# Modulation products of the first layer in four (three) column groups of 32 instead of two

## The chip, the cores and the metric

The kernel runs on one core of one Trainium2 chip. The metric is the device time in microseconds (us) of that core for one whole execution; a smaller number is better. The engines are named as the profile names them: PE (TensorE's matmuls), PEld (its weight loads), DVE (VectorE), ACT (ScalarE), POOL (GpSimd) and SP, the engine on whose queue most transfers are issued, in the order in which they are written and each after the waits of its own. Numbers such as L72 are lines of the kernel before.

## The reference

Two trunk layers of a diffusion backbone run over 128 context tokens and 512 latent tokens, 1024 features each. What matters here is the first line of a layer: every layer makes from a condition vector of 1024 features (one for the context, one for the latents) six vectors of 1024 features that shift, scale and gate its activations. These are the modulation.

```
mod_ctx = silu(c_ctx) @ w_mod[l] + b_mod[l]
mod_lat = (silu(c) @ w_mod[l] + b_mod[l])[:, None, :]
...
shift1, scale1, gate1, shift2, scale2, gate2 = split(mod, 6)
h   = (x * (1 + scale1) + shift1) @ w_in
mix = [ RWKV-7 (4 heads) | neighbourhood attention (4 heads) | GQA (8 heads) ] @ w_out
x   = LN1(alpha * x + gate1 * mix)
x   = LN2(alpha * x + gate2 * ((silu(gate) * up) @ w_ffn_out))
```

`w_mod[l]` is a matrix of 1024 x 6144 in float32, so a modulation is a product of two rows with 48 blocks of 128 columns. The rest of a layer is a dense projection, three mixers (a chunked recurrent scan and two kinds of attention), an output projection and a gated feed-forward, all in float32 accuracy.

## The kernel before

Activations lie feature-major: 128 features on the partitions, the tokens in two chunks of 320 on the free axis. A dense product is made as three products of float32r parts (`mm3`: high x high, high x low, low x high). Weights come by SP's queue in blocks of 128 x 1024 floats (`weights`, L300; transfer L306), and ACT and DVE split them in two parts (`split`, L277 and L278). All of PE's products are recorded by one helper, `Tensor.matmul` (L72), transposes by L76.

The modulation of the first layer is made in three ways. The scale and the first two shift blocks, and what comes after block 40, are dot products on DVE (`mod_block`, L194). Blocks 2 to 7 and 16 to 39 are made by `mod` (L196), which this change is about. `mod(j0, n, ...)` makes n blocks. The stationary operand is `cst`, silu(c) with each of the two condition vectors repeated 16 times, so 128 features x 32 columns. The weights stream past it as the moving operand: for each of the eight slices k of 128 features a transfer of 128 x (128 n) floats (L203), and then two products, one for each half of the n blocks, that write to PSUM partitions 0 to 31 and 32 to 63 of one bank, `ps_pv`. After the eighth, ACT copies the bank to SBUF (L210), PE transposes it block by block (L76), and DVE adds the bias into `modT` (L217). One slice with its two products is called a step below.

`mod` is called with n = 6 in `first_input` (L352), where the input of the first layer is made feature tile by feature tile as its weights come in, and with n = 4 six times in `proj_all` (L435): twice beside the projection tiles of the scan's features, and four times beside those of queries, keys and values. So there are 8 steps of 2 x 384 columns and 48 steps of 2 x 256 columns, and nothing like them in the second layer. Each of PE's float32 products has two records in the profile, so a step has four.

The order of independent work is set as the program is written out. `Tensor.now` is a running estimate of PE's time, which each product raises by a formula of its size:

```
L68  if lhsT.dtype == F32R:
L69      self.now += n / 2400
L70  else:
L71      self.now += (max(n, 100) if out.shape[0] > CH else max(n, 80) * 0.55) / 600
```

Side work is written as generators (tasks), each of which yields the time from the end of its products to where it can go on. `tick` (L255) is called every few dense products, and emits one step of each task whose time has come by that estimate; `weave` (L267) emits the tasks by themselves, the one that is ready first going first. The steps of `mod`, the eight scan jobs of a layer (`rwkv_job`, L632, in two slots: elementwise features, products within chunks, the inverse of their 16 x 16 blocks, states) and the attention are such tasks. So when the estimate changes, the order of everything that is woven after it can change, up to the end of the layer's mixers. On top of that the framework fixes each engine's own instruction list, which the engine then runs in order.

The names that the prediction uses: `md` are the matrices of a scan job, written to DRAM by ACT's queue (`md<-X`) and read back by SP's queue as 16 x 16 blocks, `BT` (L723); DVE inverts these (L775 to L788), ACT writes the transposed result `td`, and SP's queue reads it as `T` (L797) and `X` (L799), each in two transfers, one for each of the job's two heads. PE then joins the blocks, first `A` x `T`. The digit behind BT, T or X is the slot. `bias` (L937), `vw` (L927), `ks` (L951) and `qs` (L944) are loads for the attention, into space that comes free when the last dense tile of the projection is done.

Of the kernel before, what the change touches and what calls it, by code (L numbers as in the profile page):

```python
# [60 lines left out]
class Tensor:  # L61
    """TensorE's products, with a running estimate of its time (us) that orders the emission of independent work"""
# [3 lines left out]
    def matmul(self, out, lhsT, rhs, **kw):  # L66
        n = math.prod(out.shape[1:])
        if lhsT.dtype == F32R:  # L68
            self.now += n / 2400  # L69
        else:  # L70
            self.now += (max(n, 100) if out.shape[0] > CH else max(n, 80) * 0.55) / 600  # L71
        self.eng.matmul(out, lhsT, rhs, **kw)  # L72
# [11 lines left out]
class Build:  # L84
# [3 lines left out]
    def t(self, shape, name, dt=F32):  # L88
        """short-lived tile of the present phase"""
        return self.tpool.tile(shape, dt, name=name, tag="t", bufs=self.tbufs)  # L90
# [4 lines left out]
    # ---------------------------------------------------------------- set-up  # L95
# [51 lines left out]
    def mat(self, t, h):  # L147
        """the 64 x 64 matrices of one head in DRAM scratch, row first"""
        return t[:, h, 0:CH * CH].rearrange("c (s t) -> s c t", t=CH)

    def blocks(self, t):
        """their diagonal 16 x 16 blocks, one to a partition: [(chunk, head, block), row, column]"""
        b = t[0, 0, 0:1]
        return bass.AP(tensor=b.tensor, offset=b.offset, ap=[[MP // 4, 4 * NC], [CH, 16], [1, 16]])

    # ------------------------------------------------------------ modulation
    def silu_c(self):
        """silu(c) with the features on the partitions, as the stationary operand of mod"""
# [8 lines left out]
    def silu_rows(self, pool, spread):  # L167
        """silu(c) on every partition, spread there by TensorE or by the load"""
# [20 lines left out]
    def mod_block(self, l, j, c, w):  # L189
        """128 columns of the modulation as dot products on VectorE"""  # L190
# [5 lines left out]
    def mod(self, j0, n, pool, bufs=2, width=4 * P):  # L196
        """n blocks of 128 columns of the modulation of the first layer as products with the weights streamed"""
        nc = self.nc
        ps = self.psum("pv")
        w0, nb = j0 * P, n // 2 * P  # L200
        for k in range(KT):
            w = pool.tile([P, width], F32, name="wmod", tag="wmod", bufs=bufs)
            nc.sync.dma_start(w[:, 0:2 * nb], self.I["w_mod"][k * P:(k + 1) * P, w0:w0 + 2 * nb])  # L203
            yield 1.5
            for j in range(2):
# [3 lines left out]
        sb = pool.tile([P, width], F32, name="wmod", tag="wmod", bufs=bufs)[0:CH, 0:nb]  # L209
        nc.scalar.copy(sb, ps[0:CH, 0:nb])  # L210
        yield 1.0
        pt = self.psum("pv")
        for b in range(n // 2):
            self.te.transpose(pt[:, b * CH:(b + 1) * CH], sb[:, b * P:(b + 1) * P], self.ident[0:CH, 0:CH])
        src = pt[:, 0:n // 2 * CH].rearrange("p (b j w r) -> p b j w r", j=2, w=2, r=16)
        for w in range(2):
            nc.vector.tensor_tensor(  # L217
                self.modT[0][:, j0:j0 + n, w].rearrange("p (j b) -> p b j", j=2),
                src[:, :, :, w, 0],
                self.par(0, "b_mod", j0, n).rearrange("p (j b) -> p b j", j=2), ALU.add)  # L220

    def coefs(self, l, which, ln):
        """scale/bias that turn the normalised (or, without ln, the plain) x into the modulated input"""
# [15 lines left out]
    # ------------------------------------------------------ tasks on the side  # L239
    # A task is a generator of emission steps; what it yields is the time (us) from the end of the step's products  # L240
    # to where its next step can start.
# [13 lines left out]
    def tick(self):  # L255
        """beside the dense products: one step of each task that is ready"""
# [4 lines left out]
    def drain(self, *tasks):  # L261
        """emit what is left of these tasks"""
# [4 lines left out]
    def weave(self, *tasks):  # L267
        """emit the tasks, the first to be ready first, until these (or all) are done"""
# [5 lines left out]
    def split(self, src, hi, lo, scale=1.0):  # L274
        """float32r parts of src, scaled by a power of two"""
# [7 lines left out]
    def psum(self, tag):  # L283
        """PSUM: s2 holds two banks; rw and pv one"""
# [3 lines left out]
    def head_sums(self, ps, col, x, ones, starts):  # L288
        """per token (on the partitions) and head: sums of x over the head's features, for 128 tokens from each start"""
# [3 lines left out]
    def head_spread(self, ps, v, blocks):  # L293
        """v of (token, head) to all features of the head; blocks: column of v, its first token, columns of ps"""
# [5 lines left out]
    def weights(self, dram, n=1024, tag="w", dst=None):  # L300
        """load a [128, n] block of weights and split it exactly in two float32r parts"""
# [15 lines left out]
    # -------------------------------------------------------------- main flow  # L317
# [34 lines left out]
    def first_input(self, pool):  # L352
        """modulated input of the first layer, a feature tile at a time, and its products in the first projection tiles"""
# [62 lines left out]
    # ---------------------------------------------------- projection + mixing  # L416
    def proj(self, l, mts):
        """feature-major projection tiles; yields the two PSUM parts of 320 tokens of each"""
# [52 lines left out]
    def mixed(self, l):  # L471
        """the mixers' outputs as the input of the output projection, whose first tiles run beside the last scans"""
# [16 lines left out]
    def rwkv_slot(self, l, slot, pool):  # L489
        """the jobs that one set of tiles carries; the next job's features are made while the states of the one  # L490
        before are scanned"""
# [18 lines left out]
    def conv(self, l, mts):  # L510
        """short convolution over the tokens of each group"""
# [21 lines left out]
    def sigmoid(self, dst, src, bias=0.0):  # L533
        """sigmoid as 0.5 tanh(x / 2) + 0.5 (same table set as exp); bias is already halved"""
        self.nc.scalar.activation(dst, src, AF.Tanh, bias=bias, scale=0.5)

    def rwkv_begin(self, l):
# [18 lines left out]
        # normalised removal keys  # L556
# [17 lines left out]
    def rwkv_pre(self, l, ft):  # L574
        """bonus into kds, gate into v"""
# [20 lines left out]
    def rwkv_end(self, l, ft, c):  # L596
        """group norm, bonus and gate of one half of the tokens"""
# [34 lines left out]
    def rwkv_job(self, l, ft, hb, d, slot, pool):  # L632
        """One scan of two heads over five chunks, in the scan's order (backward: time reversed). Four stages:
        element-wise features; within-chunk products; inverse of their blocks; states and outputs."""
# [12 lines left out]
        def features():  # L647
# [19 lines left out]
            # FT: rho, alpha, v, alpha ; BK: beta, kappa, beta  # L667
# [31 lines left out]
        def products():  # L699
            """[beta; kappa] x [rho | alpha] of each chunk (rows swapped for the odd head)"""  # L700
            FT_, BK, W = J.FT, J.BK, J.W
            # ST: the masked products with rho, and the decayed beta, kappa in time-major order
# [18 lines left out]
            # diagonal 16x16 blocks of M^T to one partition each  # L721
# [6 lines left out]
            # time-major alpha, V and the decayed beta, kappa  # L728
# [25 lines left out]
        def inverse():  # L754
            """inverse of the blocks: 8x8 row by row from the bottom, then two of them joined"""
# [7 lines left out]
            def q8(t, i, j0, j1):  # L763
                """row i, columns j0..j1 of both diagonal 8x8 blocks"""
# [3 lines left out]
            def q8m(t, i0, i1, j0, j1):  # L768
                """transposed view [q, j, i] of rows i0..i1, columns j0..j1 of both 8x8 blocks"""
# [32 lines left out]
        def bmm(lhs, rhs, N, evac, swap=False):  # L802
            """lhs^T rhs of both heads, chunk by chunk; swap: the operands lie on the other head's partitions"""
# [8 lines left out]
        def states():  # L812
# [4 lines left out]
            # R = N V, next to alpha  # L817
            bmm(N, lambda k, c, h: RV[k, c, h, :], CH, lambda ps, c: nc.scalar.copy(AL[:, c, CH:P], ps), True)
            yield 1.17
            # X = (I - M^T)^-1 by joining blocks 16 -> 32 -> 64; T = X^T  # L820
# [11 lines left out]
            # [A' | R'] = T [alpha | R]  # L832
# [8 lines left out]
            # rho' = rho + A'^T P^T ; G^T = A'^T beta^  # L841
# [6 lines left out]
            # states at the chunks' starts  # L848
# [49 lines left out]
    # ------------------------------------------------------------- attention  # L898
    # Scores are float32r products over the stacked parts: [qh; ql] x [kh; kh], then x [kl; kl].
    def bias_rows(self, l):  # L900
        """relative position bias: every row 16 times with pitch RP, read back with pitch RP - 1"""
# [18 lines left out]
    def na_values(self, l, ft):  # L920
        """values of the window of query block j, half of the rows each: partition = (row, column)"""
# [8 lines left out]
    def na_bias(self, l, hd):  # L930
        """bias of query (r, c) and window key (7 - r', c')"""
# [9 lines left out]
    def stacked(self, dram, h, name, n, bufs):  # L941
        """one head's parts on top of each other"""
# [4 lines left out]
    def doubled(self, dram, h):  # L947
        """one head's keys, each part on both halves of the partitions"""
# [16 lines left out]
    def na_qk(self, l):  # L965
# [5 lines left out]
        for ft in range(2):  # L971
            # latent queries in the order (column block, row, column)
# [10 lines left out]
        for ft in range(2):  # L983
            # latent keys, with the softmax's scale, from the last row of the grid to the first
# [13 lines left out]
    def rope(self, x, hi, dram):  # L998
        """x * cos + partner(x) * sin on [128, 512], its float32r parts into DRAM"""
# [10 lines left out]
    def gqa_qk(self, l):  # L1010
# [27 lines left out]
        # queries: weight and rotary here, 1/rms with the softmax's scale  # L1038
# [18 lines left out]
    def values(self, l):  # L1057
        """token-major values: na_v (4 heads) and gqa_v (2 heads)"""
# [52 lines left out]
    def softmax(self, ps, n, negmax, scale, sums=None):  # L1111
        """exp(scale * ps - max) on [128, n], over its sum unless that is asked for; returns the SBUF tile"""
# [12 lines left out]
    def normed(self, o, pv, sums, view):  # L1125
        """o = the outputs of four pairs of heads over the sums (query, block, head)"""
# [7 lines left out]
    def transposed(self, p, nb):  # L1134
        """nb blocks of 128 keys of the probabilities, keys on the partitions"""
# [47 lines left out]
    def na_pair(self, l, ft, j, qk, vw, st):  # L1183
# [33 lines left out]
        if j == 3:  # L1217
            o = self.out[2 + ft][0][:, NCTX:]
            yield 1.0
            # back to the order (row, column block, column)  # L1220
# [3 lines left out]
    def gqa_pair(self, l, kv, m, t, qs, ks, st):  # L1224
        """heads 4 kv + 2 m and the next one"""
# [32 lines left out]
    # ------------------------------------------- output projection, LN, FFN  # L1258
    def gated(self, l, which, mt, c, ps, xa, z):
        """z = gate * ps + xa on one chunk of 320 tokens"""  # L1260
# [8 lines left out]
    def sums(self, c, first, z):  # L1269
        """running sums over the features of z and z^2"""  # L1270
# [330 lines left out]
```

## Time and profile before

| what | us |
|---|---|
| median of three runs | 2216.33 |
| lowest and highest of them | 2186.16, 2217.32 |
| span of the profiled execution, first to last instruction | 2193.9 |
| PE busy in it | 2090.7 (95%) |
| DVE, ACT busy | 1286.8 (59%), 901.2 (41%) |

The profiled execution is one more execution of the same program; of it the profile gives the span, and no time for what lies around it. Stages by the span's clock: input of the first layer 0 to 65, projections with the modulation beside them 65 to about 293, the rest of the mixers to 587, output projection and feed-forward to about 1110, then the second layer. In the trace a wait is put beside the instruction that ended it, and the chain of waits follows the work that ended last back from the end.

### The profile page before, as it was taken

To read this page: it belongs to the slowest core of one execution; us is meant where nothing else is said; L and a number is where in the kernel's file an instruction comes from. 1 tells how busy PE (TensorE), PEld (TensorE's weight loads), DVE (VectorE), ACT (ScalarE), POOL (GpSimd) and SP (SyncE) were. 2 spreads that over 40 slices of the span, in tenths; PEclk is the share of its full clock that TensorE was granted. 3 is DMA by queue.
4 is the path that set the end of the run, shared out by engine and by line. 5 is a ranking of instruction groups with operands and counts; after the bars stand their busy time and mean duration, and the time that the engine had idled before them with its cause. 6 is when DMAs were issued, how large, how long until landed. Compare 5 with 4: busy or idle time off the path is not lost.

```text
span 2193.9 us, 41015 instructions
## 1 busy us (share of the span) xinstructions
PE 2090.7 (95%) x16705; PEld 1883.8 (86%) x16705; DVE 1286.8 (59%) x2786; ACT 901.2 (41%) x1807; POOL 188.3 (9%) x355
## 2 busy tenths in 40 slices
PE   6989998899999999999999999989999999999997
PEld 4867776678899999999988887667779999999997
DVE  6445667576676666666766567556667523333247
ACT  3534454554564212212465445445454521221234
POOL 0011131010100000000020223100101000000000
PEclk9999998899999999999999999789999999999998
DMA  8554354111323444444431425421013122122223
GB/s 293 149 164 152 108 106 82 47 31 31 138 75 133 147 154 150 148 140 147 141 130 68 133 72 103 86 60 27 22 54 130 58 73 82 68 72 82 71 86 113
DMA packets 186594, 226.43 MB, mean 103 GB/s; under 512 B 119061, under 2 KB 128917, under 8 KB 186277
## 3 DMA queue, kind: packets, MB, share of 16 engines
q1 hardware_dynamic: 150148, 206.72, 30.7%
q0 software_dynamic: 3984, 11.90, 1.7%
q10 hardware_dynamic: 32274, 5.20, 1.4%
q8 instruction: 131, 2.15, 0.4%
q14 instruction: 57, 0.47, 0.1%
HBM read 198.37 MB, written 25.40 MB: 102 GB/s over the span
## 4 chain that ended last, share of the span: by engine, by line
PE 79%; DMA 7%; DVE 5%; issue 4%; ACT 3%; SPq 1%; POOL 0%; ACTq 0%; POOLq 0%; DVEq 0%
PE ps_s L72 43%; PE ps_rw L72 28%; PE ps_pv L72 4%; PE ps_rw L76 4%; DMA wmod<-in_w_mod 2%; DMA td<-TB 2%; DMA qs<-nqd 1%; DMA BT<-md 1%; ACT whi L277 1%; DVE wlo L278 0%; DMA c_raw<-in_cT 0%; PE ps_s L76 0%; ACT xmod L1329 0%; DMA T<-td 0%; DMA md<-X 0%
## 5 line engine op out<-in xcount | busy, mean ns | idle before, releaser
L72 PE MATMUL ps_s<-xh,whi 128*128 128x320 f32 x1312 | 419.0, 321 | 23.9 <-ACT xh L277 10.8
L72 PE MATMUL ps_s<-xh,wlo 128*128 128x320 f32 x1312 | 411.8, 314 | 3.3 <-DVE wlo L278 3.3
L72 PE MATMUL ps_s<-xl,whi 128*128 128x320 f32 x1312 | 411.3, 314 | 0.5 <-DVE xl L278 0.4
L72 PEld LDWEIGHTS ps_s<-xh,whi 128*128 128x128 f32 x1312 | 250.3, 191 | 46.7 <-ACT xh L277 12.7
L72 PEld LDWEIGHTS ps_s<-xh,wlo 128*128 128x128 f32 x1312 | 250.7, 191 | 8.1 <-DVE wlo L278 5.1
L72 PEld LDWEIGHTS ps_s<-xl,whi 128*128 128x128 f32 x1312 | 251.0, 191 | 5.1 <-issue 3.1
L278 DVE TENSOR_TENSOR wlo<-wraw,whi 128x1024 fp32r<-128x1024 f32 (+1 forms) x118 | 141.3, 1199 | 157.6 <-ACT whi L277 153.0
L72 PE MATMUL ps_s<-xh,flo 128*128 128x320 f32 x736 | 228.6, 311 | 0.0
L72 PE MATMUL ps_s<-xh,fhi 128*128 128x320 f32 x736 | 228.4, 310 | 0.0
L72 PE MATMUL ps_s<-xl,fhi 128*128 128x320 f32 x736 | 228.4, 310 | 0.0
L277 ACT CAST whi<-wraw 128x1024 fp32r<-128x1024 f32 (+1 forms) x118 | 121.2, 1028 | 250.3 <-PE ps_s L72 142.6
L277 ACT CAST fhi<-wraw 128x1024 fp32r<-128x1024 f32 (+1 forms) x82 | 83.3, 1016 | 206.0 <-PE ps_s L72 99.8
L72 PEld LDWEIGHTS ps_s<-xh,fhi 128*128 128x128 f32 x736 | 138.8, 189 | 0.1
L72 PEld LDWEIGHTS ps_s<-xl,fhi 128*128 128x128 f32 x736 | 138.8, 189 | 0.0
L72 PEld LDWEIGHTS ps_s<-xh,flo 128*128 128x128 f32 x736 | 138.7, 188 | 0.1
L278 DVE TENSOR_TENSOR flo<-wraw,fhi 128x1024 fp32r<-128x1024 f32 (+1 forms) x82 | 97.0, 1184 | 58.4 <-ACT fhi L277 58.2
L1420 ACT ACTIVATE sg<-ps_s 128x320 f32<-128x320 f32 x88 | 38.3, 435 | 188.9 <-PE ps_s L72 188.7
L1421 DVE TENSOR_TENSOR sg<-sg,ps_s 128x320 f32<-128x320 f32 x88 | 42.8, 486 | 120.4 <-ACT sg L1420 120.1
L1267 DVE SCALAR_TENSOR_TENSOR z<-ps_rw,modT,z 128x128 f32<-128x128 f32 (+2 forms) x144 | 59.0, 436 | 89.9 <-PE ps_rw L72 89.7
L72 PE MATMUL ps_rw<-hh,flo 128*128 128x320 f32 x352 | 109.1, 310 | 0.6 <-DVE flo L278 0.6
L72 PE MATMUL ps_rw<-hh,wlo 128*128 128x320 f32 x352 | 108.8, 309 | 0.1
L72 PE MATMUL ps_rw<-hh,fhi 128*128 128x320 f32 x352 | 108.8, 309 | 0.0
(394 smaller groups left out, 4508.7 us busy)
## 6 DMA issues: line engine op xcount, KB each, us to landing
wraw<-in_w_ffn_in SPq DMA_DIRECT2D x88, 512.0 KB
wmod<-in_w_modT SPq DMA_DIRECT2D x66, 512.0 KB
wraw<-in_w_in_f SPq DMA_DIRECT2D x42, 512.0 KB
wraw<-in_w_ffn_out SPq DMA_DIRECT2D x48, 448.0 KB
wmod<-in_w_mod SPq DMA_DIRECT2D x48, 256.0 KB
wraw<-in_w_out SPq DMA_DIRECT2D x16, 512.0 KB
wraw<-in_w_ffn_out SPq DMA_DIRECT2D x16, 512.0 KB
ks<-nkd SPq DMA_DIRECT2D x16, 384.0 KB
```

The source lines that it names most:

```text
L72: self.eng.matmul(out, lhsT, rhs, **kw)
L76: self.eng.transpose(out, src, ident)
L277: self.nc.scalar.copy(hi, src)
L278: self.nc.vector.tensor_tensor(lo, src, self.r32(hi), ALU.subtract)
L1267: nc.vector.scalar_tensor_tensor(z[:, a:b], ps[:, q], g, xa[:, q], ALU.mult, ALU.add)
L1420: nc.scalar.activation(sg, pg, AF.Silu)
L1421: nc.vector.tensor_tensor(sg, sg, pu, ALU.mult)
```

## The change

`mod` splits the n blocks into J groups, 4 where n is divisible by 4 and else 3, instead of 2. A step is then J products of n/J x 128 columns each, written to J x 32 partitions: 4 products of 128 columns where there were 2 of 256, and in `first_input` 3 of 256 where there were 2 of 384. The transfers are the same. The copy, the transposes and the additions follow the new layout: one transpose of 128 x 128 for n = 4 instead of two of 64 x 128, two instead of three for n = 6. And the estimate gets a formula of its own for products with 32 output partitions: 4 x 128/1800 = 0.28 us for a step where the old one gave 2 x 256 x 0.55/600 = 0.47 us (0.43 instead of 0.70 for n = 6). Comments and documentation lines are also gone from the file, so from `mod` on the lines of the changed kernel are 4 higher, and those of `Tensor` 2 higher.

```diff
@@ class Tensor: matmul
         if lhsT.dtype == F32R:
             self.now += n / 2400
+        elif out.shape[0] == 32:
+            self.now += n / 1800
         else:
...
@@ def mod(self, j0, n, pool, bufs=2, width=4 * P):
         ps = self.psum("pv")
-        w0, nb = j0 * P, n // 2 * P
+        J = 4 if n % 4 == 0 else 3
+        w0, nb, R = j0 * P, n // J * P, J * 32
         for k in range(KT):
             w = pool.tile([P, width], F32, name="wmod", tag="wmod", bufs=bufs)
-            nc.sync.dma_start(w[:, 0:2 * nb], self.I["w_mod"][k * P:(k + 1) * P, w0:w0 + 2 * nb])
+            nc.sync.dma_start(w[:, 0:n * P], self.I["w_mod"][k * P:(k + 1) * P, w0:w0 + n * P])
             yield 1.5
-            for j in range(2):
+            for j in range(J):
                 self.te.matmul(ps[32 * j:32 * j + 32, 0:nb], self.cst[:, k].rearrange("p a b -> p (a b)"),
                                w[:, j * nb:(j + 1) * nb], start=(k == 0), stop=(k == KT - 1), skip_group_check=True)
         yield 0.5
-        sb = pool.tile([P, width], F32, name="wmod", tag="wmod", bufs=bufs)[0:CH, 0:nb]
-        nc.scalar.copy(sb, ps[0:CH, 0:nb])
+        sb = pool.tile([P, width], F32, name="wmod", tag="wmod", bufs=bufs)[0:R, 0:nb]
+        nc.scalar.copy(sb, ps[0:R, 0:nb])
         yield 1.0
         pt = self.psum("pv")
-        for b in range(n // 2):
-            self.te.transpose(pt[:, b * CH:(b + 1) * CH], sb[:, b * P:(b + 1) * P], self.ident[0:CH, 0:CH])
-        src = pt[:, 0:n // 2 * CH].rearrange("p (b j w r) -> p b j w r", j=2, w=2, r=16)
+        for b in range(n // J):
+            self.te.transpose(pt[:, b * R:(b + 1) * R], sb[:, b * P:(b + 1) * P], self.ident[0:R, 0:R])
+        src = pt[:, 0:n // J * R].rearrange("p (b j w r) -> p b j w r", j=J, w=2, r=16)
         for w in range(2):
             nc.vector.tensor_tensor(
-                self.modT[0][:, j0:j0 + n, w].rearrange("p (j b) -> p b j", j=2),
+                self.modT[0][:, j0:j0 + n, w].rearrange("p (j b) -> p b j", j=J),
                 src[:, :, :, w, 0],
-                self.par(0, "b_mod", j0, n).rearrange("p (j b) -> p b j", j=2), ALU.add)
+                self.par(0, "b_mod", j0, n).rearrange("p (j b) -> p b j", j=J), ALU.add)
```

On PE a step beside the projection tiles, about 97 us into the kernel, stood like this before (the row in the middle; `ps_s` are accumulators of the dense tiles):

```order
L72 MATMUL ps_s_672<-xl_157,whi 128x320
L72 MATMUL ps_s_672<-xh_156,wlo 128x320
L72 MATMUL ps_pv<-wmod,cst 32x256 x2
L72 MATMUL ps_s_757<-xl_155,whi 128x320
L72 MATMUL ps_s_757<-xh_154,wlo 128x320
```

and now stands like this:

```order
L74 MATMUL ps_s_685<-xl_157,whi 128x320
L74 MATMUL ps_s_685<-xh_156,wlo 128x320
L74 MATMUL ps_pv<-wmod,cst 32x128 x4
L74 MATMUL ps_s_778<-xh_154,wlo 128x320
L74 MATMUL ps_s_778<-xh_154,whi 128x320
```

The step stays in one piece and at about the same place between the dense products; it has four products of half the columns.

From about 120 us to 580 us the order on all engines differs. One place on SP's queue, where the loads of the attention begin (about 288 us), stood like this before:

```order
L797 DMA T0_3046<-td1_1013 64x5x64 x2
L799 DMA X0_3045<-xd1_1010 64x5x64 x2
L937 DMA bias_2951<-rpx0_1055 128x8x32 x4
L937 DMA bias_2960<-rpx0_1055 128x8x32 x4
L927 DMA vw_2969<-vd0_2437 128x1x128 x8
L951 DMA ks_2978<-nkd0_1128 64x2x768 x2
L951 DMA ks_2981<-nkd0_1128 64x2x768 x2
L944 DMA qs_2984<-nqd0_1127 128x1x512
L944 DMA qs_2986<-nqd0_1127 128x1x512
L723 DMA BT1_3319<-md_3158 40x16x16
L951 DMA ks_3905<-nkd0_1128 64x2x768 x2
L944 DMA qs_3911<-nqd0_1127 128x1x512
```

and now like this:

```order
L803 DMA X0_3125<-xd1_1048 64x5x64 x2
L801 DMA T0_3126<-td1_1051 64x5x64
L941 DMA bias_3012<-rpx0_1093 128x8x32 x4
L941 DMA bias_3021<-rpx0_1093 128x8x32 x4
L931 DMA vw_3030<-vd0_2504 128x1x128 x8
L955 DMA ks_3039<-nkd0_1165 64x2x768 x2
L955 DMA ks_3042<-nkd0_1165 64x2x768 x2
L948 DMA qs_3045<-nqd0_1164 128x1x512
L948 DMA qs_3047<-nqd0_1164 128x1x512
L801 DMA T0_3126<-td1_1051 64x5x64
L955 DMA ks_3973<-nkd0_1165 64x2x768 x2
L948 DMA qs_3979<-nqd0_1164 128x1x512
```

The second of the two reads of T0, of the third scan job, has moved from ahead of the 22 loads of the attention to behind them; and the next two loads each of `ks` and `qs` now stand ahead of the read of BT1, which follows two rows further on.

On PE the products that read that T0 stood before in one piece, behind the output products of another job:

```order
L72 MATMUL ps_rw_3104<-ST1_2012,RV1_2232 64x64 x2
L72 MATMUL ps_rw_3104<-RHO1_2233,S1_2917 64x64 x2
L72 MATMUL ps_rw_3127<-T0_3046,A00_2543 64x64 x10
L76 MATMUL ps_rw_3140<-ident_78,prob_3018 128x128
L76 MATMUL ps_rw_3144<-ident_78,prob_3033 128x128
```

and now stand in two pieces, the first head's first product ahead of some attention of the context tokens and the other nine behind it:

```order
L74 MATMUL ps_rw_3205<-T0_3126,A00_2679 64x64
L78 MATMUL ps_rw_3228<-ident_78,prob_3109 128x128
L74 MATMUL ps_pv_3270<-pT_3196,vc_2502 64x128
L74 MATMUL ps_rw_3231<-RV1_2386,ST1_2177 64x64 x2
L74 MATMUL ps_rw_3231<-S1_3134,A11_2966 64x64 x2
L74 MATMUL ps_rw_3242<-kds_1209,rk_3132 128x320
L74 MATMUL ps_pv_3270<-pT_3227,vc_2502 64x128
L74 MATMUL ps_s2_3377<-gkc_1624,gqc_1770 128x128
L74 MATMUL ps_s2_3274<-gkc_1624,gqc_1770 128x128
L74 MATMUL ps_s2_3452<-gkc_1624,gqc_1770 128x128
L74 MATMUL ps_rw_3205<-T0_3126,A00_2679 64x64 x9
```

The output products of the other job have gone behind these, and the other nine need the second read of T0.

Between the last dense tile of the projection and the second read's products the new order has 4 products `pT` x `vc`, 4 products `gkc` x `gqc` and 2 transposes of `prob` more than before, and of the scan's small products about as many in another selection (44 before; 43 now, one of them the first head's `T0` x `A00`).

## Rows read from the trace of the kernel before

**Rows 1.** The page: span, and PE's busy time (share, instructions).

```profile
span 2193.9 us, 41015 instructions
...
PE 2090.7 (95%) x16705; PEld 1883.8 (86%) x16705; DVE 1286.8 (59%) x2786; ACT 901.2 (41%) x1807; POOL 188.3 (9%) x355
```

**Rows 2.** Stretches: length, busy of five engines, PE's clock, DMA share, GB/s.

```profile
130.00:200.00 70.00, 66.63 (x468) 50.70 (x466) 34.10 (x75) 25.61 (x57) 10.09 (x17) 1.00 0.55 170
...
330.00:351.00 21.00, 18.18 (x122) 13.80 (x123) 11.03 (x42) 6.79 (x18) 0.33 (x2) 0.51 0.13 35
...
259.00:587.00 328.00, 306.01 (x3307) 242.06 (x3308) 214.74 (x600) 169.81 (x397) 49.46 (x74) 0.93 0.28 65
1309.00:1651.00 342.00, 320.66 (x3336) 252.78 (x3337) 217.42 (x607) 173.09 (x404) 47.27 (x74) 0.90 0.26 58
```

**Rows 3.** Groups of PE by shape: all records of the modulation's products.

```profile
L72 PE MATMUL ps_pv<-wmod,cst 128*32 128x256 f32 x192 | 32.7, 390 | 4.8 <-DMA wmod<-in_w_mod 3.2 <-issue 1.2 <-ACT cx L524 0.4
L72 PE MATMUL ps_pv<-wmod,cst 128*32 128x384 f32 x32 | 7.6, 585 | 2.6 <-DMA wmod<-in_w_mod 2.6
```

**Rows 4.** Chain of waits, 30 to 270 us: start, length, what, records.

```profile
35.27 0.77 PE ps_pv L72 x4
...
73.76 0.56 PE ps_pv L72 x4
...
174.08 5.91 DMA wmod<-in_w_mod
...
262.34 0.56 PE ps_pv L72 x4
```

**Rows 5.** Timeline of PEld and PE around one step at 81 us.

```profile
81.08 0.14 PEld L72 LDWEIGHTS ps_pv<-wmod,cst 128*32 128x32 f32 x4 [0.19 <-issue]
...
81.09 0.63 PE L72 MATMUL ps_pv<-wmod,cst 128*32 128x256 f32 x4
81.64 0.42 PE L72 MATMUL ps_s<-xh,whi 128*128 128x320 f32 x1
```

**Rows 6.** Timeline of DVE, first input: the addition behind `mod`, idle before it.

```profile
40.14 0.24 DVE L217 TENSOR_TENSOR modT<-ps_pv,pp 128x6 f32<-128x6 f32 x2 [8.48 <-PE ps_pv L76]
```

**Rows 7.** Groups of ACT by shape: the copies behind `mod`.

```profile
L210 ACT COPY wmod<-ps_pv 64x256 f32<-64x256 f32 x6 | 2.2, 364 | 6.5 <-PE ps_pv L72 6.5
...
L210 ACT COPY wmod<-ps_pv 64x384 f32<-64x384 f32 x1 | 0.5, 473 | 8.7 <-PE ps_pv L72 8.7
```

**Rows 8.** Timeline of SP's queue (SPq), attention loads: start and length of issue.

```profile
292.17 7.23 SPq L937 DMA_DIRECT2D bias<-rpx  x8
...
309.01 2.51 SPq L944 DMA_DIRECT2D qs<-nqd  x2
```

**Rows 9.** Timeline of PE: products with T, and the end of an idle time.

```profile
304.21 0.75 PE L72 MATMUL ps_rw<-T,A 64*64 64x64 f32 x20
...
331.77 0.45 PE L72 MATMUL ps_pv<-pT,vc 128*64 128x128 f32 x1 [5.29 <-DVE tmpB L778]
```

**Rows 10.** Chain of waits from 304 us, the last row in layer 1.

```profile
304.96 0.37 PE ps_rw L76 x2
305.33 0.36 PE ps_pv L72 x2
...
312.60 0.11 PE ps_s L72
...
321.86 9.39 DMA BT<-md
...
403.82 2.48 DMA T<-td
...
1491.90 7.52 DMA BT<-md
```

**Rows 11.** Groups of PE by shape, 330 to 351 us.

```profile
L72 PE MATMUL ps_s<-ks,qs 128*128 128x256 f32 x12 | 3.7, 457 | 0.0
```

**Rows 12.** The same form on PE, 423 to 460 us.

```profile
L72 PE MATMUL ps_s<-ks,qs 128*128 128x256 f32 x18 | 4.0, 304 | 0.0
```

## The prediction, made before the changed kernel ran

> **What bounds the kernel now.** I read the page first. PE is busy 2090.7 of 2193.9 us [rows 1], so the time is PE's work plus about 103 us in which it stands, and an edit that takes work from PE counts in full wherever PE's products are what the chain of waits runs through. So the next view was the chain through the stages in which `mod` works. The first step at n = 4 on it starts at 73.76, the last at 262.34, each a piece of four records of 0.56 us; a step at n = 6 is a piece of 0.77 [rows 4]. Counted piece by piece, the chain holds 14 of the n = 4 steps between 65 and 116 us, 13 between 130 and 200, 14 between 200 and 270: 41 of 48. The other 7 lie where PE waits for `wmod` itself; one such wait, at 174.08, is 5.91 us long [rows 4], and the DMA engines are 0.55 busy in that stretch [rows 2]. All records of `mod` have 32.7 + 7.6 us of busy time [rows 3], which runs two at a time. That is the whole of what a better layout can touch: 48 x 0.56 + 8 x 0.77 = 33 us of the path, and in it the change can win some fraction.
>
> Then I looked for what the order change touches, since the estimate feeds the tasks' times: the order differs from 120 to 580 us. There the stretches, SP's queue and PE's idle times matter, and those I take up below.
>
> **The two halves already run side by side.** Two products of 256 columns, four records, start at 81.09 and the next dense product starts at 81.64; their four weight loads take 0.14 us together from 81.08 on, so the last begins while the first product runs [rows 5]. The path pays 0.56 us for them, though one record lasts 390 ns [rows 3] and four after each other would be 1.56.
>
> **Direct part: the steps.** From 256 to 384 columns a step grows by 0.77 - 0.56 = 0.21 us [rows 4]. If that is the price of 128 columns per group, a step of 128 columns costs 0.56 - 0.21 = 0.35, with four groups at once as with two. Against it stand four more weight loads: at 0.14/4 = 0.035 us each [rows 5], eight take 0.28, still under 0.35, so they need not set the pace; I charge 0.01. So 0.20 us per n = 4 step, 41 x 0.20 = 8.2 us. The seven steps behind `wmod` transfers I take at nothing: a shorter step there makes PE wait longer for the same transfer. They would give 1.4 at most, if the transfers started that much earlier.
>
> In the first input, DVE sits idle 8.48 us until PE has finished `mod` [rows 6], so there the latency counts. Four of the eight steps lie on the chain behind the last late transfer. From 2 x 384 to 3 x 256 each goes from 0.77 to 0.56: 4 x 0.21 = 0.84. The copy shrinks from 473 ns (384 columns) to what 256 columns take, 364 [rows 7]: 0.11. Together 0.95.
>
> The six other copies shrink too, but dense products run beside them: nothing, and it cannot be over their 2.2 us [rows 7]. Transposes go from 15 to 8. Two of 128 x 128 take 0.37 us of the chain [rows 10], so seven fewer are worth at most 7 x 0.19 = 1.3; as each has twice the rows I take nothing. Both bounds stay in the range.
>
> Direct sum: 8.2 + 0.95 = 9.2 us gained; 12 if the bounds all pay, nothing if the groups do not overlap (rival 3).
>
> **The Trainium skill on this.** "TensorE: Matmul & The Clock Gate", Part 3 (packing small matmuls, measured speedup) gives 2.38 times for three column tiles of 512, 0.79 of the ideal three. An estimate by that: four tiles would gain 3.2 times, so of a step's 2 x (0.56 - 0.14) = 0.84 us of streaming there would remain 0.26 plus 0.14 = 0.40 instead of 0.35, and the direct sum would be some 2 us smaller. The trace shows two groups only, so no row here decides between them.
>
> **Indirect part: the new order.** The place that I can price is the third scan job's second read of T0. Before, it stood ahead of the attention's loads; now it stands behind 22 of them on SP's queue. Before, the first of them is issued at 292.17, and the last, `qs`, at 309.01 for 2.51 us [rows 8], so it would begin at 311.5. Such a read takes 2.48 us where it is on the chain [rows 10]: 314.0. PE took up T x A at 304.21 [rows 9]. On the clock of before the products would wait 314.0 - 304.2 = 9.8 us. Against this the new order puts more in front of them: 4 products `pT` x `vc` (0.36 for two, so 0.72), 4 of `gkc` x `gqc` (0.11 each, 0.44) and 2 transposes (0.37) [rows 10], 1.5 us. The wait is then 8.3. All of it shifts equally with the direct gain, since the loads wait for the last dense tile's space. Queued behind the waiting product on PE are X x N, the next job's FT x BK and so its `md`, BT and inverse: what follows moves as a whole, nothing else can step in. Bounds: 0 if the read's place does not matter, 9.8 if the added products are already waited for.
>
> Something comes back at the next place. BT<-md took 9.39 us with `ks` and `qs` loads issued just behind it, and 7.52 at its place in the second layer [rows 10]; PE's 5.29 us idle ends behind it [rows 9]. With the loads done early, BT should take the lower of these: 1.9 back. Bounds: 0, and 5.29 if the attention products now standing there cover the whole.
>
> The clock is the unknown. After that idle of 5.29 us the granted clock is 0.51 for 21 us [rows 2, 9], near the lower of PE's two levels (1.2 against 2.4 GHz). The same product of 256 columns takes 457 ns there and 304 at full clock [rows 11, 12], so a third of the 18.18 us busy [rows 2] is lost: 6.1 us. A wait of 8.3 is longer than 5.29, so I expect a slow stretch behind it; but the slow stretch of before at 330 to 351 may then go, as its idle time shrinks. I take these two as one for one: 0, with 6.1 as the other end (both occur), and -6.1 (neither).
>
> **Sum.** -9.2 + 8.3 - 1.9 + 0 = -2.8 us. On the profiled execution that is a span of 2191.1 for 2193.9. The page gives no time around its span, and the change touches neither start nor end, so I apply the -2.8 to the median: 2216.33 - 2.8 = 2213.5. The median lies 22.4 over the span, and the three runs are 31 apart; a change under 2% (44 us) is about what a measurement of this kernel cannot tell from none.
>
> **Rivals.**
> 1. The stall does not come, since the new order elsewhere lets the dense tiles end, or the read come, sooner relative to PE. Then -9.2: 2207.1. For it: all 22 loads wait on one tile's space, a small lead would free all. Against: SP is in order and the read stands behind them.
> 2. Slower: the stall comes, BT's wait stays, and both idle times bring a slow clock: -9.2 + 8.3 + 6.1 = +5.2, 2221.5. It decides once PE's second idle time stays near 5.29 [rows 9]. For it: BT's `md` is written by products queued behind the stall, so it is late by as much. Against: the new order has `ks` x `qs` products ready there.
> 3. The change does not do what it says: four groups run two by two. Then an n = 4 step stays at 2 x 0.28 = 0.56, an n = 6 step takes two rounds of 256, 1.12 for 0.77, so 4 x 0.35 - 0.11 = +1.3; with +8.3 - 1.9 this is +7.7, 2224.0. Against: two groups show no mutual hindrance [rows 5]. An extreme of it: all four in turn, 0.21 each plus 0.14, 0.98 for 0.56, which is 41 x 0.42 = 17.2, and 4 x (3 x 0.42 + 0.14 - 0.77) = 2.5 in the first input; with the order's +6.4, +26.1, 2242.4.
>  The skill's rule behind the extreme ("TensorE: Matmul & The Clock Gate", Part 3, the mechanism): a weight load overlaps running products only where the row groups differ, and column groups share all rows. Here the trace disagrees: four loads within 0.14 us of 81.08 beside a product from 81.09 [rows 5].
> 4. The new order is better elsewhere by more than this stall costs. The same mixers take 328 us in this layer and 342 in the second, where the order is another [rows 2]: 14 us by order and clock alone. By half of that: -9.2 - 7 = -16.2, 2200.1; by all, 2193.
>
> **How the numbers follow.** Forecast 0.34 (own range 2207 to 2220), rival 1 0.22, rival 2 0.18, rival 3 0.10 (0.02 of it the extreme), rival 4 0.16. Range 2178 to 2230: up past rivals 2 and 3 with a few us of other reordering, down past rival 4 and towards the lowest run of before, 2186, with its gain. The extreme and larger swings of the order are left out. Faster by over 2% (under 2172) needs several gains of rival 4's size: 0.03; slower by over 2% (over 2260.7) needs the extreme and a bad order: 0.03; within, 0.94.
>
> **What would show it.** Right: steps of eight records of 128 columns at about 0.35 us on the chain, three of 256 at 0.56 in the first input; the dense tiles end about 9 us earlier; PE waits some 8 us for T<-td near 300 us, with a clock near 0.5 behind it, and less for BT. Wrong: steps at 0.5 or more (rival 3), no wait for T (rival 1), two slow stretches between 290 and 350 (rival 2), or the stretch from the dense tiles' end to 587 shorter by more than 5 us (rival 4). A difference after the mixers of the first layer, where the order is the same, would be none of these.

## The result, and the profile after

| | before | changed | ratio, 95% interval |
|---|---|---|---|
| first comparison, median us (runs) | 2203.89 (4) | 2213.91 (4) | 1.0102 [1.0058, 1.0145] |
| second comparison (E8) | 2196.52 (17) | 2225.71 (4) | 1.0140 [1.0112, 1.0167] |
| span of the profiled execution | 2193.9 | 2212.5 | |

The changed kernel is slower by 1.0 to 1.4%, by these ratios some 22 to 31 us (the medians of the table are 10 and 29 us apart), where a gain of 2.8 was forecast. Its profiled execution took 2214.35 us in all, so 1.9 us lie around the span; the profiled execution of before, with its 2193.9, stands near the median of 2196.9 of the 29 runs that were made of that kernel beside E1 to E4, and the 2216.33 of the first three runs was a high value.

The page, the span and the busy times, answers to [rows 1]:

```profile
span 2212.5 us, 41399 instructions
...
PE 2085.5 (94%) x16906; PEld 1886.9 (85%) x16906; DVE 1287.0 (58%) x2786; ACT 903.9 (41%) x1809; POOL 190.5 (9%) x355
```

PE is 5 us less busy in a span that is 18.6 longer: the loss is idle time. First the part that the change is about. The groups by shape, the counterpart of [rows 3]:

```profile
L74 PE MATMUL ps_pv<-wmod,cst 128*32 128x128 f32 x384 | 23.2, 299 | 2.5 <-DMA wmod<-in_w_mod 2.0 <-ACT cx L528 0.4
L74 PE MATMUL ps_pv<-wmod,cst 128*32 128x256 f32 x48 | 6.4, 481 | 1.0 <-DMA wmod<-in_w_mod 1.0
```

The timeline of PEld and PE around one step, as [rows 5]:

```profile
79.86 0.16 PEld L74 LDWEIGHTS ps_pv<-wmod,cst 128*32 128x32 f32 x8 [0.19 <-issue]
...
79.86 0.43 PE L74 MATMUL ps_pv<-wmod,cst 128*32 128x128 f32 x8
80.21 0.41 PE L74 MATMUL ps_s<-xh,whi 128*128 128x320 f32 x1
```

Eight weight loads take 0.16 us, all eight records lie within 0.43, and the next dense product starts 0.35 after the first. Four column groups run side by side. The addition behind `mod` in the first input, on DVE, as [rows 6]:

```profile
39.22 0.24 DVE L221 TENSOR_TENSOR modT<-ps_pv,pp 128x6 f32<-128x6 f32 x2 [7.16 <-PE ps_pv L78]
```

It starts 0.92 us earlier than before. At the first attention load the kernel is 7.9 us ahead (284.28 for 292.17). SP's queue from there, as [rows 8]; a length here is that of the issue, with what SP waits in it:

```profile
283.59 0.57 SPq L801 DMA_DIRECT2D T<-td  x1
284.28 7.93 SPq L941 DMA_DIRECT2D bias<-rpx  x8
292.25 5.34 SPq L931 DMA_DIRECT2D vw<-vd  x8
297.63 2.65 SPq L955 DMA_DIRECT2D ks<-nkd  x4
300.32 3.87 SPq L948 DMA_DIRECT2D qs<-nqd  x2
304.23 7.98 SPq L801 DMA_DIRECT2D T<-td  x1
```

The second read of T0 is issued behind all 22 loads, and issuing it alone takes SP 7.98 us. On PE's timeline this is what comes of it:

```profile
299.83 0.79 PE L74 MATMUL ps_s<-gkc,gqc 64*128 64x128 f32 x2 [1.64 <-ACT prob L1123]
...
323.71 1.32 PE L74 MATMUL ps_rw<-T,A 64*64 64x64 f32 x18 [23.08 <-DMA T<-td]
...
429.77 0.44 PE L74 MATMUL ps_rw<-T,A 64*64 64x64 f32 x2 [9.80 <-DMA T<-td]
```

PE waits 23.08 us for the read, and the other engines do next to nothing meanwhile. The same stretch of time, first in the kernel before, then in the changed one (columns as in [rows 2]):

```profile
300.63:323.71 23.08, 22.35 (x277) 16.66 (x277) 18.62 (x65) 15.41 (x54) 8.48 (x12) 1.00 0.58 120
```

```profile
300.63:323.71 23.08, 0.00 (x1) 0.01 (x1) 0.54 (x2) 0.06 (x1) 0.77 (x3) 0.50 0.56 119
```

PE had 277 records there and has one; DVE, ACT and POOL stand too, and the granted clock is at its lower level. Only the DMA engines work as before, 0.56 busy for 0.58. So by the profile's time the kernel goes from 7.9 us ahead to behind in one place, and what follows moves with it: the products with T start 19.5 us later than before (323.71 for 304.21), the first dense product behind the mixers 21.6 later (596.16 for 574.59), and the span is 18.6 longer.

### The profile page after: what moved, and what is told of

It reads as the page before. It is cut to its first block, busy times and chain, and to the rows that moved or that the text cites. A ratio compares the mean times of both kernels' runs of the same rounds, so it can differ in the third digit from the quotient of the medians.

```text
span 2212.5 us, 41399 instructions
## 1 busy us (share of the span) xinstructions
PE 2085.5 (94%) x16906; PEld 1886.9 (85%) x16906; DVE 1287.0 (58%) x2786; ACT 903.9 (41%) x1809; POOL 190.5 (9%) x355
## 4 chain that ended last, share of the span: by engine, by line
PE 78%; DMA 7%; issue 5%; DVE 5%; ACT 3%; SPq 2%; POOL 0%; ACTq 0%; POOLq 0%; DVEq 0%
PE ps_s L74 43%; PE ps_rw L74 27%; PE ps_pv L74 4%; PE ps_rw L78 4%; DMA td<-TB 2%; DMA T<-td 1%; DMA wmod<-in_w_mod 1%; DMA xa<-in_xT 1%; SPq L955 1%; ACT whi L281 0%; SPq L931 0%; DVE wlo L282 0%; DMA c_raw<-in_cT 0%; ACT xmod L1333 0%; DMA BT<-md 0%
## 5 line engine op out<-in xcount | busy, mean ns | idle before, releaser
L74 PE MATMUL ps_s<-ks,qs 128*128 128x256 f32 (+1 forms) x384 | 103.8, 379 | 8.6 <-DMA qs<-gqd 4.4
```

## The experiments

Theory A: the column groups give what their steps show, and the loss is the one read behind the loads. Its rivals: any new order loses (B), the groups cost something unseen (C), the wait would only move (D), the estimate's error costs (E).

**E1 and E11, the column groups alone.** The estimate's new branch is taken out:

```diff
-        elif out.shape[0] == 32:
-            self.now += n / 1800
```

> The changed kernel without the new line of the estimate, so the column groups alone; its order differs from before at far fewer places, and both reads of the third scan job's T0 stand ahead of the attention's loads again. Theory A (the column groups give what their steps show, and the changed kernel's loss is the read behind the loads): no wait for T near 300 us, about 8 us faster than before. Theory B (every new order loses, whichever read stands where): 0 to 20 us slower than before in spite of it. Theory C (the column groups have a price that their steps don't show): not faster, with the dense tiles' end no earlier than 290 us.

Measured 2188.13 (13 runs), ratio 0.9952 [0.9928, 0.9976], 10.5 us faster than before; once more as E11:

> The column groups with the old estimate once more, beside the two others on one chip: 0.3 to 0.7% faster than before.

0.9967 [0.9943, 0.9992], 7 us faster by the ratio. In E1's trace (its longest execution, 2209.23 us; E11's, of 2187.96, has the same reads and waits, some 2 us earlier) SP's queue has both reads of that T0 ahead of the loads, and PE's timeline has no wait for them; what is left near there is the wait behind BT that the kernel before had as well:

```profile
275.20 1.78 SPq L801 DMA_DIRECT2D T<-td  x2
...
287.38 7.47 SPq L941 DMA_DIRECT2D bias<-rpx  x8
```

```profile
326.66 0.45 PE L74 MATMUL ps_pv<-pT,vc 128*64 128x128 f32 x1 [5.03 <-DVE tmpB L782]
...
402.01 0.44 PE L74 MATMUL ps_rw<-T,A 64*64 64x64 f32 x2 [8.55 <-DMA T<-td]
```

C falls: without the new estimate the groups gain. B falls as far as it says that every new order loses.

**E2, the new estimate alone.** Two halves as before, under the new formula:

```diff
-        J = 4 if n % 4 == 0 else 3
+        J = 2
```

> The changed kernel with J = 2, so the two halves of before under the new estimate. In its order both reads of T0 stand ahead of the loads. Theory A: no wait for T near 300 us, so within 7 us of before either way. Theory B' (the lower estimate of the modulation products by itself makes a bad order): 15 to 28 us slower than before, as the changed kernel and without the steps' gain.

2200.23 (12 runs), 1.0011 [0.9984, 1.0038]. Neither part loses alone; only together do they give the order with the late read.

**E3, the one read moved.** All of the change stays, and the two reads of that T0 go to POOL's queue:

```diff
-                nc.sync.dma_start(J.T[hs[h]], self.mat(tdr, h))
+                (nc.gpsimd if l == 0 and q == 1 else nc.sync).dma_start(J.T[hs[h]], self.mat(tdr, h))
```

> The changed kernel with the two reads of that one T0 (layer 0, third scan job) issued on POOL's queue, where they don't stand behind the attention's loads. Theory A: the 23.1 us idle of PE before T x A goes or shrinks under 3 us, and the kernel gets 17 to 23 us faster than the changed one, so 5 to 12 us faster than before. Theory D (the wait only moves: the next job's matrices or the attention's loads end last there): the idle time shows up within the next 60 us before another tile, and under 8 us are won.

2194.06 (12 runs), 0.9965 [0.9937, 0.9993], so 7.7 us faster than before and, by the ratios, 30 to 38 faster than the changed kernel (20 to 32 by the medians), more than the 17 to 23 expected. POOL's and PE's timelines:

```profile
284.36 1.40 POOL L801 DMA_DIRECT2D T<-td  x2
```

```profile
294.88 0.80 PE L74 MATMUL ps_rw<-T,A 64*64 64x64 f32 x20
...
318.64 0.58 PE L74 MATMUL ps_s<-ks,qs 128*128 128x256 f32 x1 [2.91 <-DMA qs<-nqd]
```

The reads land 4.6 us after their issue (median of the DMA view), the products run at 294.88, with no wait, and PE's next idle time above 2 us is one of 2.91 for the loads themselves. D falls: the wait is won, not moved. The edit is not the one read alone, though: both reads of this T0 are now issued with the first load, and the order woven around them differs too (all 20 records of the products stand in one piece again).

**E9, the reverse.** To the kernel of E1 one small copy is added, which holds that read back until the second `qs`, the last of the 22 loads, has landed (`self.late` is its tile):

```diff
+            if l == 0 and q == 1:
+                nc.gpsimd.tensor_copy(J.T[hs[1], 0, 0:1], self.r32(self.late[hs[1], 0:1]))
             for h in range(2):
                 nc.sync.dma_start(J.T[hs[h]], self.mat(tdr, h))
```

> The column groups with the old estimate, plus one copy of 64 values from qs into the second half of that T0 before its read overwrites it, so that this one read waits until the attention's loads have landed; the order around it follows as in the changed kernel. Theory A (the read's place is enough): PE waits 20 us or more for T near 300 us, 18 to 28 us slower than the same kernel without the copy, so 0.4 to 0.9% slower than before. Theory F (the changed kernel's loss needs the rest of its order): under 10 us slower than without the copy.

2212.49 (8 runs), 1.0067 [1.0036, 1.0098]: 22 us over E11 by the ratios, on the same chip; the profiled executions of the two are 16.6 us apart. SP, POOL and PE:

```profile
286.23 7.54 SPq L943 DMA_DIRECT2D bias<-rpx  x8
...
323.21 0.60 SPq L803 DMA_DIRECT2D T<-td  x1
```

```profile
323.00 0.19 POOL L801 COPY T<-qs 64x1 f32<-64x1 f32 x1 [12.84 <-DMA qs<-nqd]
```

```profile
325.87 1.29 PE L74 MATMUL ps_rw<-T,A 64*64 64x64 f32 x18 [15.96 <-DMA T<-td]
```

The second `qs` has landed at 323.00, 36.8 us after the first load's issue; the read behind it takes 2.66 us, and PE starts on T 39.6 us after the first load, for 39.4 in the changed kernel. So there too the read costs what the batch takes to land. PE's wait is shorter than expected, 15.96 us, since PE came to it later, at 309.91. From 295 us on it had worked at the lower clock:

```profile
295.00:309.91 14.91, 14.09 (x70) 8.50 (x70) 7.25 (x25) 6.37 (x21) 5.97 (x10) 0.51 0.69 145
```

So a read that comes this late is enough for a loss of this size, and in E3, where it comes early, there is no loss. F falls. Neither edit isolates the read altogether: in E9 SP stands until the copy is done, so the loads behind the read are late too.

**E4 and E7, what the read waits for.** The loads ahead of it are made smaller: in E4 the bias loads to an eighth, in E7 the first four `ks` loads to a half.

```diff
-            nc.sync.dma_start(bias[:, j], bass.AP(tensor=b.tensor, offset=b.offset + off, ap=[[RP - 1, P], [16 * (RP - 1), 8], [1, NA_N]]))
+            w = 1 if l == 0 and hd < 2 else 8
+            if w == 1:
+                nc.vector.memset(bias[:, j], 0.0)
+            nc.sync.dma_start(bias[:, j, 0:w], bass.AP(tensor=b.tensor, offset=b.offset + off, ap=[[RP - 1, P], [16 * (RP - 1), w], [1, NA_N]]))
```

> The changed kernel with the first two heads' bias loads of layer 0 cut to one of eight rows each (same 8 transfers, an eighth of their bytes and of their 128-byte pieces; the rest of the bias is left at zero, so that part of the attention's bias is not computed). The second read of T0 still stands behind the loads. Theory A1 (the read waits for what is in flight ahead of it): the wait for T falls from 23 us to 10 to 16. Theory A2 (it waits for something else, the write of td or a semaphore of its own): it stays within 2 us of 23.

```diff
+            w = 1 if self.nk < 2 else 2
...
+            self.nc.sync.dma_start(self.r32(t[u * CH:(u + 1) * CH, 0:w]), dram[0:w, h * CH:(h + 1) * CH, :].rearrange("a p n -> p a n"))
```

> The changed kernel with the first four loads of ks in layer 0 cut to half their bytes (the other half of these keys is left at zero, so that part of the attention's scores is not computed): 0.79 MB less ahead of the late read of T0, with as many transfers. Theory A1 (the wait is the bytes in flight ahead of the read): the wait for T falls from 23 us by 4 to 8. Theory A2 (the number of transfers or the issues set it): it stays within 2 us of 23.

The wait fell to 17.08 us in E4 and to 10.10 in E7. Against the expectation E4 lies between its two theories and E7, with 13 us less, outside both of its own; and the waits themselves mislead: in E7 PE came later. The clean measure is from the issue of the first load to PE's start on T. The DMA view of the changed kernel between 284 and 330 us gives the sizes:

```profile
ks<-nkd SPq DMA_DIRECT2D x6, 384.0 KB
bias<-rpx SPq DMA_DIRECT2D x8, 128.0 KB
qs<-nqd SPq DMA_DIRECT2D x4, 256.0 KB
vw<-vd SPq DMA_DIRECT2D x8, 64.0 KB
```

Ahead of the read stand 8 x 128 + 8 x 64 + 4 x 384 + 2 x 256 = 3584 KB (the other `ks` and `qs` come behind it). The first load, the read's issue and PE's start, first in E4, then in E7:

```profile
286.16 0.61 SPq L931 DMA_DIRECT2D vw<-vd  x1
...
302.20 7.64 SPq L801 DMA_DIRECT2D T<-td  x1
...
321.23 1.32 PE L74 MATMUL ps_rw<-T,A 64*64 64x64 f32 x18 [17.08 <-DMA T<-td]
```

```profile
287.33 7.79 SPq L942 DMA_DIRECT2D bias<-rpx  x8
...
305.81 4.94 SPq L802 DMA_DIRECT2D T<-td  x1
...
322.16 1.32 PE L74 MATMUL ps_rw<-T,A 64*64 64x64 f32 x18 [10.10 <-DMA T<-td]
```

| | KB ahead | first load to T x A, us | of it up to the read's issue, behind it |
|---|---|---|---|
| changed kernel | 3584 | 323.71 - 284.28 = 39.4 | 19.95, 19.48 |
| changed again (E8) | 3584 | 324.18 - 284.57 = 39.6 | 20.07, 19.54 |
| E4 | 2688 | 321.23 - 286.16 = 35.1 | 16.04, 19.03 |
| E7 | 2816 | 322.16 - 287.33 = 34.8 | 18.48, 16.35 |

A fifth to a quarter fewer bytes bring the read 4.3 to 4.6 us forward, about 5 to 6 us per 1000 KB. So what stands ahead of the read does make it late (A1); if the rest scaled alike, the bytes would make up some 17 to 21 of the 39 us, which no run shows. Where the time is won differs: in E4, with an eighth of the bias pieces, mostly in the issue of the loads ahead, in E7 mostly behind the read's own issue. What the rest hangs on, such as the number of transfers or the loads issued behind the read, was not tried. There is one execution of each (2210.55 and 2226.01 us), which says nothing on the time.

**E5, E6 and E8, other estimates.** With n/1600 to n/2000 the order has the read behind the loads, with n/1300 to n/1500 and from n/2200 on ahead of them. One of each side was run, with the changed kernel again beside them.

```diff
-            self.now += n / 1800
+            self.now += n / 1500
```

> The changed kernel with n/1500 in the estimate, 0.34 us for a step of four products, about what a step takes on the chain of the changed kernel (0.36). In its order both reads of that T0 stand ahead of the attention's loads. Theory A (the place of this read decides): no wait for T near 300 us, 5 to 12 us faster than before, about as the column groups with the old estimate. Theory B (orders differ at random, this read is one of many): anything from 10 us faster to 20 slower than before.

> The changed kernel with n/2200 in the estimate, 0.23 us for a step, farther from the truth than the 0.28 of the change. In its order both reads of that T0 stand ahead of the loads again. Theory A: 5 to 12 us faster than before in spite of the worse estimate. Theory E (the estimate's error is what costs, the lower the worse): 10 us or more slower than before, no better than the changed kernel.

> The changed kernel itself, beside the others on one chip: 0.5 to 1.5% slower than before, as in its first comparison, and some 20 us slower than the two other estimates by theory A.

E5: 1.0030 [1.0006, 1.0054]; E6: 1.0094 [1.0069, 1.0120]; E8 is in the first table. Here A misses: both have the read ahead and no wait for it, yet neither gains the 5 to 12 us. The late read is the changed kernel's loss, and an order can lose in other ways, so B holds that far. In E5 the first load of the attention starts only 0.6 us earlier than before (292.17):

```profile
291.55 7.69 SPq L941 DMA_DIRECT2D bias<-rpx  x8
```

So the steps' gain was lost ahead of it; how, is not shown. The chain of waits, from 100 to 300 us, holds 18.2 us of `wmod` transfers, 7.5 more than in the changed kernel (10.7), but the kernel before has more than both, 24.4.

In E6 PE waits for the reads of later scan jobs instead:

```profile
403.98 0.44 PE L74 MATMUL ps_rw<-T,A 64*64 64x64 f32 x2 [13.73 <-DMA T<-td]
...
505.77 0.45 PE L74 MATMUL ps_rw<-T,A 64*64 64x64 f32 x2 [6.01 <-DMA T<-td]
```

The same place in the kernel before, as one line of PE's timeline:

```profile
406.44 0.44 PE L72 MATMUL ps_rw<-T,A 64*64 64x64 f32 x2 [7.74 <-DMA T<-td]
```

The first wait has grown by 6.0 us, and the second is new among the waits over 2 us. E6's time is what theory E foretold; but E2, whose estimate is farthest off (0.28 us for a step of 0.55), loses nothing, so the error by itself is not the cause. Nor does the better estimate win: n/1500 is nearest to the step's 0.36 us, and the old formula, with 0.47 for it, gave the fastest kernels. Whether those two waits are all of E6's loss stays open.

**E10, the groups only beside the projection.** Old estimate, and J = 2 in the first input:

```diff
-        J = 4 if n % 4 == 0 else 3
+        J = 4 if n % 4 == 0 else 2
```

> Old estimate; four column groups in the calls of n = 4, the two halves of before in the first input. By the sum: 8.2 of the 9.2 us, so 0.3 to 0.5% faster than before. On the side: if the idle time of 5.4 us near 121 us (3.7 in before) comes from the first input's three groups, it is back at 3.7 here; if from the steps beside the projection, it stays.

2183.20 (7 runs), 0.9946 [0.9926, 0.9967], 11.9 us faster than before: the best ratio of all, though E1 and E11 overlap with it. The idle time near 121 us stays:

```profile
121.78 2.50 PE L74 MATMUL ps_rw<-FT,BK 64*128 64x128 f32 x12 [5.35 <-DVE BK L697]
```

So it does not come from the first input's groups. E2, with halves everywhere, lacks it, so it belongs to the steps beside the projection; why they bring it was not followed. The 3.7 us of before is another wait, of a dense product for ACT's split (3.65, at 124.10).

## Why the prediction was wrong

- **The steps: right.** Forecast 0.35 us for four groups, the start of the next product stands 0.35 after the first (0.35 or 0.36 in most pieces of the chain). In the first input 0.95 was forecast, 0.92 measured. The estimate worked out from the Trainium skill, "TensorE: Matmul & The Clock Gate", Part 3 (measured speedup), was 0.40, so the groups here overlap better than that. The Trainium skill's rule there (the mechanism), that a weight load overlaps running products only where the row groups differ, stood behind rival 3's extreme of 0.98; the eight loads in 0.16 us, beside products that start with the first of them, disagree. Rival 3 is out.
- **The direct sum: right, within what the runs can tell.** 9.2 us forecast (8.2 for E10); 10.5, 7 and 11.9 us in E1, E11 and E10, the whole kernel timed. The lead of 7.9 at the first load fits too but is no clean measure, since the order has a part in it as well: E2, without the groups, is 4.5 us ahead there, E5, with them, 0.6. Nor do the steps alone change: the transfers of `wmod` on the chain from 100 to 300 us, whose change was taken at nothing, fell from 24.4 us to 10.7, more than the whole lead, so other pieces of the chain grew.
- **The place and mechanism of the loss: right.** The read behind 22 loads, and PE waiting for it. Rival 1 is out.
- **The price of it: wrong, and with it the sign.** The step that failed is "such a read takes 2.48 us where it is on the chain: 314.0". That row was a read that had SP's queue to itself. Here it stands behind 3584 KB and takes 19.43 us, and PE starts on it 39.4 us after the first load's issue instead of 314.0 - 292.17 = 21.8: 17.6 us more. PE came to it at 300.63, where 304.21 - 7.9 + 1.5 = 297.8 had been forecast, 2.8 later. 8.3 + 17.6 - 2.8 = 23.1, the measured wait. That an issue's end is not a landing stood in the trace of before: BT, whose issue takes 0.31 us, took 9.39, and I read only its excess over 7.52 as the price of the loads issued beside it.
- **What comes back at BT: undersized.** 1.9 forecast; no wait of over 2 us behind BT is left on PE, of 5.29 [rows 9]. But T x A further on waits 9.80 us, for 7.74, so 3.2 came back of the two.
- **The clock: taken at nothing, and near it.** The lower level came, but for the most part in the wait itself, where PE has nothing to lose; behind the wait it lasts to 330, and the slow stretch of before at 330 to 351 (0.51 [rows 2]) is gone:

```profile
323.71:330.00 6.29, 5.71 (x69) 4.66 (x69) 1.75 (x4) 0.00 (x0) 0.00 (x0) 0.50 0.14 47
330.00:351.00 21.00, 20.19 (x216) 14.62 (x215) 11.65 (x44) 11.19 (x37) 1.93 (x2) 0.99 0.10 26
```

Added up in stretches of 1 us, from the first attention load to the first dense product behind the mixers, PE worked 34.1 us at the lower level before, 37.0 in the changed kernel and 28.7 in E8, and stood idle 20.6, 44.9 and 45.2. The loss in these executions is idle time, not the clock.

- **Rivals 2 and 4.** Rival 2 had the sign, at +5.2 us, but not by its mechanism: the second wait went, and the first was nearly three times its size. In size the extreme of rival 3, +26.1, lies nearest to the 22 to 31 us, by chance: its steps are not there. That orders differ by 10 us and more (rival 4's premise) shows in E6, and in E5 against E1, against the change and not for it.
- **Luck.** The changed kernel's first median, 2213.91, stands 0.4 us from the forecast 2213.5. That is chance: the forecast was a change of -2.8 from a median of before that was high, and against all the runs of before that were made beside it the change is a loss, by a ratio of 1.0102.

## What to carry to other kernels

A read that a scheduler moves behind a batch of loads on one queue costs the batch's landing, not the read's own time: take it from the issue of the first load to the landing of the last, where such a batch is on the trace (36.8 us in E9). A change of a cost estimate is a change of the whole order behind it: run the layout with the old estimate and the estimate with the old layout, and look on each queue for what short reads on the critical path now stand behind. A closer estimate need not give a better order.

## What the runs showed of the hardware

Four column groups of 128 columns each took 0.35 us where two of 256 took 0.55. A read of 80 KB that took 2.48 us from its issue in the kernel before (403.82), and 2.66 in E9 once the batch had landed, took 19.43 us from the start of its issue behind 3584 KB, 7.98 of them before SP could go on to its next transfer:

```profile
304.23 19.43 DMA T<-td
```

In E9 the granted clock was 0.51 from 295 to 309.91 us, where PE worked 14.09 of 14.91 us and had no idle time over 0.82 us. PE reached the late read later than in the changed kernel (309.91 for 300.63), and the wait shown on the trace was 15.96 us for 23.08, though PE started on T as long after the first load (39.6 us for 39.4). So the price of such a read is better taken from the batch's first issue than from the wait.
